# Retention scores inside halves of 256 tokens, with the first half's state carried to the second

## The chip, the core and the metric

The kernel runs on one core of one Trainium2 chip. The metric is the device time of one execution in microseconds (us). The kernel before was timed three times: 1077.37, 1076.7 and 1073.35 us, median 1076.7 us. One execution was also taken by the profiler. It took 1071.51 us, with a span of 1069.7 us from its first to its last recorded instruction, and every duration below is from that execution.

The core has five engines that work side by side, each through its own instructions in the order in which the program holds them: PE (matrix products into PSUM banks of 128x512), DVE (vector work), ACT (activations and scaled copies), POOL and SP (here almost only issuing DMAs). An instruction whose inputs are not ready holds up everything behind it on its own engine.

## The reference

One step of a decoder layer: a prompt of 512 tokens and eight sampled sequences of one token. The input is normalised, projected by one wide matrix, and goes through two branches, retention (RetNet) and RWKV-7, which are gated, merged, projected and normalised. The change touches retention alone, with 4 heads, keys of 256 and values of 512 elements:

```
def chunk(s, qkv):
    qc, kc, vc = qkv
    inner = jnp.einsum('bhid,bhjd->bhij', qc, kc) * dmask
    o = jnp.einsum('bhij,bhjv->bhiv', inner, vc) + jnp.einsum('bhid,bhdv->bhiv', qc * q_dec, s)
    s = chunk_dec * s + jnp.einsum('bhjd,bhjv->bhdv', kc * k_dec, vc)
    return s, o
```

The reference scans chunks of 128. Any chunk length gives the same result: a token's output is a decayed sum over all earlier tokens, either through scores against their keys or through a state that has summed them up. Wanted are the outputs `o` (normalised per token and head, then gated) and the last state `s`. All is float32.

## The kernel before

**Precision.** A float32 product is made of three products in the faster type F32R: each operand is split into a high part and the rest (`hi`, `lo`), and hi·hi, hi·lo and lo·hi are summed in PSUM. ACT makes the high part as a copy, DVE the rest as a difference.

**Weights.** `fetch` (L140) loads 512 KB of weights into a tile `raw`, of which there are three buffers. `weights` (L145) splits it: `whi` on ACT (L147), `wlo` on DVE (L148), two buffers each. So the split of one block of weights must wait until PE is through with the block two before it, and a load until all readers of the block three before it are done. `proj` (L160) then runs 48 products, 24 for each half of the tokens, into one of four banks named `ph`.

**One head of retention** (loop at `for h in range(H)`), in the order in which the code is written:

- `rope` for k and q: four blocks of weights, each followed by copies to `rx`; then on DVE three operations of 520 columns for each half of the head's dimension (L810 to L812) and a split.
- v: four blocks of weights of another shape (L838, 24 products of 512 columns each, into the four `ph` banks that stay open for all four). After the second and the fourth block the eight sampled tokens' v (`vsm`, L831) is made from the *unsplit* tiles `raw` of two blocks, so these two buffers stay taken until then. `vsm` lies in the only buffer of the bank `po`.
- Scores (L863): four blocks of 128 keys, block jt against queries 128·jt to 511, hence 512, 384, 256 and 128 columns wide; each is multiplied by the decay table `dmask` on DVE (L866) and split.
- Keys transposed back and scaled by their decay (`kt`, `dhi`, `dlo`, L882 to L884).
- `sampled`: the eight sampled sequences' states come from HBM by POOL's DMAs in tiles `tS` (four buffers, 1 MB each), are updated on ACT and DVE (L764, L765), go out again, and four rows of products end in the bank `po` (L770).
- Gates (`gs`), four blocks of weights.
- Outputs (L910): for each of four blocks of queries the products over all earlier key blocks, 30 in all; the final state (`st`, L921) from all four key blocks, 24 products; then the norm's factors `ort` by `rsqrt`, a chain of 13 small DVE instructions; `ot` transposed (L928) and gated into `gs` (L930); in the last step `sampled_out` makes a second factor `os` by the same chain, scales `po` by it on ACT into `on` (L782), which frees the bank `po`, and transposes `on` (`yas`, L785).

All banks but `ph` and `po` rotate through three buffers. Beside this, DVE works off RWKV's triangular solve (`tm` and `M`, L623 and L625, 62 pairs of up to 992 columns), which `advance` hands out by a running account of due work, and later the sampled RWKV heads.

**What sets the order.** The code is not issued as written. The tile framework plays the program through a model of the engines (`schedule_with_timeline_sim`) and puts each engine's instructions in the order in which they come up there, by readiness and by the order of the code. `tc.issue_after` and `after` add a few fixed precedences. Each edit can thus move instructions of any engine far from it.

Where a stage follows retention, RWKV's eight chunks run as chains of short products (L1025, L1034, L1040, L1043) among projections that fill the time.

Of the kernel before, what the change touches and what calls it, by code (L numbers as in the profile page):

```python
# [18 lines left out]
HT = 256  # L19
# [22 lines left out]
def constants():  # L42
    import numpy as np

    f = np.float32
    c = {}
    inv = (10000.0 ** (-np.arange(128) / 128)).astype(f)
    pos = np.concatenate([np.arange(T), np.full(B8, 4096)]).astype(f)
    ang = (pos[:, None] * inv[None, :]).astype(f)
    c["cos"] = np.ascontiguousarray(np.cos(ang).T.astype(f))  # L50
    c["sin"] = np.ascontiguousarray(np.sin(ang).T.astype(f))
    j = np.arange(128)[:, None]
    i = np.arange(T)[None, :]
    c["dmask"] = np.stack([np.where(i >= j, GAM[h] ** np.maximum(i - j, 0) / 16.0, 0.0) for h in range(H)], 1).astype(f)
    jj = np.arange(T).reshape(4, 128).T
    c["kdec"] = np.stack([GAM[h] ** (511 - jj) / 16.0 for h in range(H)], 1).astype(f)
    s = np.arange(64)[:, None]
    t = np.arange(64)[None, :]
    le, lt = (s <= t).astype(f), (s < t).astype(f)
    ev = np.concatenate([np.concatenate([le, -0.5 * lt], 1), np.concatenate([le, lt], 1)], 0)  # L60
    od = np.concatenate([np.concatenate([-0.5 * lt, le], 1), np.concatenate([lt, le], 1)], 0)
    c["gmask"] = np.concatenate([ev, od, ev, od], 1)
    r = np.ones((128, NT), f)
    r[:, 0:T:C] = 0.0
    r[:, T:] = 0.0
    c["reset"] = r
    ind = np.zeros((128, NPAIR, 16), f)
    for p in range(NPAIR):
        ind[:64, p, 2 * p] = 1.0
        ind[64:, p, 2 * p + 1] = 1.0  # L70
    c["ind"] = ind
    c["indT"] = np.ascontiguousarray(np.concatenate([ind.transpose(2, 1, 0)] * 2, 0))
    bd = np.zeros((128, 128), f)
    bd[:64, :64] = 1.0
    bd[64:, 64:] = 1.0
    c["bdiag"] = bd
    return c


def body(tc, A, O, dbg=None, upto="Z"):  # L80
# [11 lines left out]
    with es:  # L92
# [516 lines left out]
        pB.tile([128, 1280], F32R, tag="ihi", name="ihi")  # L609
        cos = pB.tile([128, NT], F32, tag="cos", name="cos")  # L610
        pool.dma_start(cos, A["cos"])
        sin = pB.tile([128, NT], F32, tag="sin", name="sin")
# [175 lines left out]
                              ps.rearrange("p (i b r) -> p i b r", i=4, b=4)[:, :, :, 0:2],  # L788
                              gs8[:, hs_, :].rearrange("p i (g b) -> p i b g", g=2), ALU.mult)

        OFF = [0, 512, 896, 1152]
        GBC = [0, 0, 0, 4, 8]
        for h in range(H):
            roped = {}
# [56 lines left out]
            qhi, qlo, _ = roped["q"]  # L851
            khi, klo, kf = roped["k"]

            dmask = pB.tile([128, T], F32, tag="dmask", name="dmask", bufs=1)
            (sp if h else pool).dma_start(dmask, A["dmask"][:, h, :])
            ihi = pB.tile([128, 1280], F32R, tag="ihi", name="ihi")
            ilo = pB.tile([128, 1280], F32R, tag="ilo", name="ilo")
            for jt in range(4):
                n = T - 128 * jt
                ps = bank("sc")  # L860
                seq = [(i, a_, b_) for i in range(2) for a_, b_ in ((khi, qhi), (khi, qlo), (klo, qhi))]
                for x, (i, a_, b_) in enumerate(seq):
                    pe.matmul(ps[:, 0:n], a_[:, i, 128 * jt:128 * jt + 128], b_[:, i, 128 * jt:T],  # L863
                              start=(x == 0), stop=(x == 5))
                s_ = pB.tile([128, T], F32, tag="s_", name="s_", bufs=1)
                dve.tensor_tensor(s_[:, 0:n], ps[:, 0:n], dmask[:, 0:n], ALU.mult)  # L866
# [12 lines left out]
            for jt in range(4):  # L879
                ps = bank("kt")  # L880
                for i in range(2):
                    pe.transpose(ps[:, 128 * i:128 * i + 128], kf[i][:, 128 * jt:128 * jt + 128], ident)  # L882
                act.activation(dhi[:, jt, :], ps[:, 0:256], AF.Copy, scale=kdec[:, h, jt:jt + 1])
                dve.scalar_tensor_tensor(dlo[:, jt, :], ps[:, 0:256], kdec[:, h, jt:jt + 1], dhi[:, jt, :], ALU.mult, ALU.subtract)  # L884
            po = sampled(h)

            gs = []
# [13 lines left out]

            oss = pB.tile([128, 4], F32, tag="oss", name="oss", bufs=2)
            ort = pB.tile([128, 4], F32, tag="ort", name="ort", bufs=2)
            ot = [x[:, i, :] for x in (pB.tile([128, 2, DV], F32, tag=t, name="ot") for t in ("qhi", "qlo")) for i in range(2)]
            for it in range(4):
                ps = bank("o")
                seq = [(jt, a_, b_) for jt in range(it + 1) for a_, b_ in ((ihi, vhi), (ihi, vlo), (ilo, vhi))]
                for x, (jt, a_, b_) in enumerate(seq):
                    o_ = OFF[jt] + 128 * (it - jt)
                    pe.matmul(ps, a_[:, o_:o_ + 128], b_[:, jt, :], start=(x == 0), stop=(x == len(seq) - 1))  # L910
                o = ot[it]
                act.activation(o, ps, AF.Square, accum_out=oss[:, it:it + 1])
                act.activation(o, ps, AF.Copy)
            rsqrt(ort, oss, 1.0 / DV, NORM_EPS)
            for it in range(4):
                act.activation(ot[it], ot[it], AF.Copy, scale=ort[:, it:it + 1])
            for i in range(2):
                ps = bank("st")
                seq = [(jt, a_, b_) for jt in range(4) for a_, b_ in ((dhi, vhi), (dhi, vlo), (dlo, vhi))]
                for x, (jt, a_, b_) in enumerate(seq):  # L920
                    pe.matmul(ps, a_[:, jt, 128 * i:128 * i + 128], b_[:, jt, :], start=(x == 0), stop=(x == 11))  # L921
# [408 lines left out]
```

## Time and profile before

| what | value |
|---|---|
| times of the kernel before | 1077.37, 1076.7, 1073.35 us |
| profiled execution, its time and its span | 1071.51 us, 1069.7 us |
| granted PE clock over the span | 0.992 |
| PE busy | 1042.0 us (97%), 8932 products |
| DVE busy | 785.2 us (73%) |
| ACT busy | 494.8 us (46%) |
| stage of retention | about 270 to 710 us of the span |
| in it, PE and DVE busy | 436.83 and 353.36 us of 440 |

A product's recorded time overlaps that of the next, since they are pipelined. What a product costs in a row of products is the distance from its start to the next one's start. The same holds in small for DVE: where instructions stand back to back, the next starts some 0.06 to 0.1 us before the recorded end of the one before. Rows named "waits" say who waited for whom; in the timeline, a bracket behind an instruction says how long its engine stood idle before it.

### The profile page before, as it was taken

How to read it: one execution, taken by the hardware profiler on the slowest of the kernel's cores; microseconds unless marked ns; L12 is line 12 of the kernel's file. 1: busy time of each engine (PE TensorE's matmuls, PEld its weight loads, DVE VectorE, ACT ScalarE, POOL GpSimd, SP SyncE). 2: the span in 40 equal slices, each digit the busy share in tenths (PEclk: the TensorE clock that was granted, in tenths of full speed). 3: DMA queues.
4: the chain of work that ended last, by engine and by line, in shares of the span. 5: the costliest groups of instructions: out<-in, count | busy, mean ns of one | idle time of the engine just before them, and what ended most of it. 6: DMA issues, size and time to landing. Idle time of an engine off the chain costs nothing.

```text
span 1069.7 us, 22049 instructions
## 1 busy us (share of the span) xinstructions
PE 1042.0 (97%) x8932; PEld 974.8 (91%) x8932; DVE 785.2 (73%) x1429; ACT 494.8 (46%) x973; POOL 79.5 (7%) x139
## 2 busy tenths in 40 slices
PE   7999999999999999999999999998999999999995
PEld 6999989999879788987989889898999999999995
DVE  6647989884499699949894698864777755666875
ACT  6744565544464543373445333354323224334554
POOL 2000110100300200010010000110001100000000
PEclk8999999999999999999999999999999999999998
DMA  5623488788943943493288633969996649643222
GB/s 182 179 80 99 122 191 223 188 246 228 330 160 90 327 146 99 144 319 103 86 310 229 230 115 112 328 198 330 309 283 214 171 145 302 206 119 100 81 59 81
DMA packets 239224, 199.45 MB, mean 186 GB/s; under 512 B 58988, under 2 KB 203225, under 8 KB 237970
## 3 DMA queue, kind: packets, MB, share of 16 engines
q1 hardware_dynamic: 225586, 149.60, 47.7%
q0 software_dynamic: 13376, 48.17, 13.2%
q8 instruction: 70, 1.15, 0.4%
q14 instruction: 32, 0.26, 0.1%
q10 hardware_dynamic: 160, 0.27, 0.1%
HBM read 137.70 MB, written 60.00 MB: 185 GB/s over the span
## 4 chain that ended last, share of the span: by engine, by line
PE 85%; DMA 6%; DVE 3%; ACT 2%; issue 1%; SPq 1%; POOL 0%; DVEq 0%; POOLq 0%; ACTq 0%
PE ph L160 58%; PE phv L838 8%; PE o L910 3%; PE st L921 2%; PE sc L863 1%; PE po L770 1%; PE g L506 1%; PE UO L1025 1%; DMA raw<-in_w_ple_gate_dram 1%; DMA raw<-in_w_in_dram 1%; DMA yalo<-YAd 1%; DMA BKt<-BKd 1%; DMA MBd<-mg 1%; PE vb L762 1%; PE vsm L831 1%
## 5 line engine op out<-in xcount | busy, mean ns | idle before, releaser
L160 PE MATMUL ph<-hhi,whi 128*128 128x256 f32 (+2 forms) x1296 | 370.5, 286 | 0.9 <-ACT hhi L282 0.4
L160 PE MATMUL ph<-hlo,whi 128*128 128x256 f32 (+2 forms) x1296 | 369.4, 285 | 0.2 <-DVE hlo L283 0.2
L160 PE MATMUL ph<-hhi,wlo 128*128 128x256 f32 (+2 forms) x1296 | 368.8, 285 | 0.5 <-DVE wlo L148 0.5
L160 PEld LDWEIGHTS ph<-hhi,whi 128*128 128x128 f32 x1296 | 244.2, 189 | 6.1 <-issue 1.7
L160 PEld LDWEIGHTS ph<-hhi,wlo 128*128 128x128 f32 x1296 | 245.0, 189 | 2.2 <-DVE wlo L148 0.7
L160 PEld LDWEIGHTS ph<-hlo,whi 128*128 128x128 f32 x1296 | 244.5, 189 | 1.9 <-DVE hlo L283 0.7
L147 ACT ACTIVATE whi<-raw 128x1024 fp32r<-128x1024 f32 x135 | 142.9, 1059 | 208.9 <-PE ph L160 154.2
L148 DVE TENSOR_TENSOR wlo<-raw,whi 128x1024 fp32r<-128x1024 f32 x135 | 164.8, 1221 | 86.4 <-ACT whi L147 85.4
L160 PE MATMUL ph<-yalo,whi 128*128 128x256 f32 (+1 forms) x256 | 72.4, 285 | 0.0
L160 PE MATMUL ph<-yahi,whi 128*128 128x256 f32 (+1 forms) x256 | 72.2, 284 | 0.0
L160 PE MATMUL ph<-yahi,wlo 128*128 128x256 f32 (+1 forms) x256 | 71.9, 285 | 0.0
L623 DVE TENSOR_TENSOR tm<-M 128x62 f32<-128x62 f32 (+30 forms) x62 | 52.9, 853 | 0.6
L625 DVE TENSOR_TENSOR M<-M,tm 128x62 f32<-128x62 f32 (+30 forms) x62 | 52.8, 852 | 0.6
L838 PE MATMUL phv<-whi,hhi 128*128 128x512 f32 x128 | 51.5, 403 | 0.0
L838 PE MATMUL phv<-whi,hlo 128*128 128x512 f32 x128 | 50.5, 395 | 0.0
L160 PEld LDWEIGHTS ph<-yalo,whi 128*128 128x128 f32 x256 | 48.1, 188 | 0.3
L160 PEld LDWEIGHTS ph<-yahi,whi 128*128 128x128 f32 x256 | 48.1, 188 | 0.2
L160 PEld LDWEIGHTS ph<-yahi,wlo 128*128 128x128 f32 x256 | 47.8, 188 | 0.3
L838 PE MATMUL phv<-wlo,hhi 128*128 128x512 f32 x128 | 46.8, 395 | 0.5 <-DVE wlo L148 0.5
L765 DVE SCALAR_TENSOR_TENSOR tS<-vb,ks,tS 128x512 f32<-128x512 f32 x64 | 44.1, 742 | 3.3 <-PE vb L762 3.3
L764 ACT ACTIVATE tS<-tS 128x512 f32<-128x512 f32 x64 | 35.0, 620 | 12.5 <-DMA tS<-in_state_ret_dram 12.4
L215 ACT ACTIVATE mg<-ph 128x256 f32<-128x256 f32 (+1 forms) x48 | 17.7, 378 | 41.2 <-PE ph L160 20.6
(454 smaller groups left out, 2120.0 us busy)
## 6 DMA issues: line engine op xcount, KB each, us to landing
raw<-in_w_in_dram SPq DMA_DIRECT2D x97, 512.0 KB, 5.0
tS<-in_state_ret_dram POOLq DMA_DIRECT2D x16, 1024.0 KB, 8.4
out_dram<-tS POOLq DMA_DIRECT2D x16, 1024.0 KB, 9.9
KR<-KRd SPq DMA_DIRECT2D x8, 1024.0 KB, 9.5
raw<-in_w_down_a_dram SPq DMA_DIRECT2D x16, 512.0 KB, 6.8
KRd<-KRS SPq DMA_DIRECT2D x16, 256.0 KB, 4.5
KRd<-GM SPq DMA_DIRECT2D x16, 256.0 KB, 4.8
BKt<-BKd SPq DMA_DIRECT2D x8, 512.0 KB, 9.9
```

The source lines that it names most:

```text
L147: cp = act.activation(hi, raw, AF.Copy)
L148: sb = dve.tensor_tensor(lo, raw, hi, ALU.subtract)
L160: m_ = pe.matmul(ps[:, 0:c1 - c0], w[:, k, :], r[:, k0 + k, c0:c1], start=(x == 0), stop=(x == n_ - 1))
L215: act.activation(g[:, c0:c1], ps, fn, scale=scale)
L506: ms = [pe.matmul(gs[2 * q + hh][:, c * 128:(c + 1) * 128], BK[hs_, 4 * q + c, :], KRS[hs_, 4 * q + c, :], start=True, stop=True) for q in ...
L623: dve.tensor_tensor(tv, M[:, 0:s, s:s + 1].to_broadcast([128, s, n]), M[:, s:s + 1, s + 1:C].to_broadcast([128, s, n]), ALU.mult)
L625: dve.tensor_tensor(M[:, 0:s, s + 1:C], M[:, 0:s, s + 1:C], tv, ALU.add)
L764: act.activation(S[:, b, :], S[:, b, :], AF.Copy, scale=GAM[h])
L765: last = dve.scalar_tensor_tensor(S[:, b, :], vb, ks[:, h, i, 4 * g + b:4 * g + b + 1], S[:, b, :], ALU.mult, ALU.add)
L838: m_ = pe.matmul(vps[jt], r[:, 2 * j + k, 128 * jt:128 * jt + 128], w_[:, k, :], start=(j == 0 and k == 0 and x == 0), stop=(j == 3 and k ...
L910: pe.matmul(ps, a_[:, o_:o_ + 128], b_[:, jt, :], start=(x == 0), stop=(x == len(seq) - 1))
L921: pe.matmul(ps, a_[:, jt, 128 * i:128 * i + 128], b_[:, jt, :], start=(x == 0), stop=(x == 11))
```

## The change

Scores are made inside halves of 256 tokens only: key blocks 0 and 1 against queries 0 to 255, blocks 2 and 3 against queries 256 to 511, so the four score blocks are 256, 128, 256 and 128 columns wide. The tables and tiles shrink to match (`dmask` 256 columns, `ihi` and `ilo` 768).

What the second half's queries get from the first half's keys now goes through the first half's state. Right behind the keys' transposes, 12 products (bank `st`) sum up key blocks 0 and 1; ACT copies the high part (`shi`), DVE makes the rest (`slo`, in the buffers `ro_k` of the rope's first step). At the outputs, 12 products (`oc`) of the two later query blocks with this state come first; ACT scales them by the query's decay (`qdec`, a new table loaded once) into `ot`. The output products are then 3, 6, 3 and 6. For the two later blocks DVE adds the inner part from PSUM to `ot` and ACT squares that into a scratch tile (`sqo`), where before ACT squared and copied straight from PSUM. The final state's products take key blocks 2 and 3 only, and DVE adds `shi` and `slo` in two steps, in the place of one copy on ACT. The tile `st` has one buffer, shared with rope's second step and the masked scores.

```diff
-        OFF = [0, 512, 896, 1152]
+        OFF = [0, 256, 384, 640]
+        qdec = pB.tile([128, H, 2], F32, tag="qdec", name="qdec")
+        pool.dma_start(qdec, A["qdec"])
...
             for jt in range(4):
-                n = T - 128 * jt
+                n = HT - 128 * (jt % 2)
...
-                    pe.matmul(ps[:, 0:n], a_[:, i, 128 * jt:128 * jt + 128], b_[:, i, 128 * jt:T],
+                    pe.matmul(ps[:, 0:n], a_[:, i, 128 * jt:128 * jt + 128], b_[:, i, 128 * jt:128 * jt + n],
...
+            vk = ((dhi, vhi), (dhi, vlo), (dlo, vhi))
+            shi = pB.tile([128, 2, DV], F32R, tag="shi", name="shi")
+            slo = [pB.tile([128, NT], F32R, tag="ro_k", name="slo", bufs=2)[:, 0:DV] for _ in range(2)]
+            for i in range(2):
+                ps = bank("st")
+                for x, (jt, (a_, b_)) in enumerate((jt, ab) for jt in range(2) for ab in vk):
+                    pe.matmul(ps, a_[:, jt, 128 * i:128 * i + 128], b_[:, jt, :], start=(x == 0), stop=(x == 5))
+                act.activation(shi[:, i, :], ps, AF.Copy)
+                dve.tensor_tensor(slo[i], ps, shi[:, i, :], ALU.subtract)
             po = sampled(h)
...
+            for it in (2, 3):
+                pss[it] = ps = bank("oc")
+                seq = [(i, a_, b_) for i in range(2) for a_, b_ in ((qhi, shi[:, i, :]), (qhi, slo[i]), (qlo, shi[:, i, :]))]
...
+            for it in (2, 3):
+                act.activation(ot[it], pss[it], AF.Copy, scale=qdec[:, h, it - 2:it - 1])
             for it in range(4):
                 ps = bank("o")
-                seq = [(jt, a_, b_) for jt in range(it + 1) for a_, b_ in ((ihi, vhi), (ihi, vlo), (ilo, vhi))]
+                seq = [(jt, a_, b_) for jt in range(it // 2 * 2, it + 1) for a_, b_ in ((ihi, vhi), (ihi, vlo), (ilo, vhi))]
...
-                act.activation(o, ps, AF.Square, accum_out=oss[:, it:it + 1])
-                act.activation(o, ps, AF.Copy)
+                if it < 2:
+                    act.activation(o, ps, AF.Square, accum_out=oss[:, it:it + 1])
+                    act.activation(o, ps, AF.Copy)
+                else:
+                    dve.tensor_tensor(o, o, ps, ALU.add)
+                    sqo = pB.tile([128, NT], F32, tag="ro_q", name="sqo", bufs=1)
+                    act.activation(sqo[:, 0:DV], o, AF.Square, accum_out=oss[:, it:it + 1])
...
-                seq = [(jt, a_, b_) for jt in range(4) for a_, b_ in ((dhi, vhi), (dhi, vlo), (dlo, vhi))]
...
+                for x, (jt, (a_, b_)) in enumerate((jt, ab) for jt in (2, 3) for ab in vk):
...
-                act.activation(st, ps, AF.Copy)
+                dve.tensor_tensor(st, ps, shi[:, i, :], ALU.add)
+                dve.tensor_tensor(st, st, slo[i], ALU.add)
```

The scheduler's order changes with it, from the first head's scores on. Three places matter below. In the rows of the changed kernel the line numbers are higher, by 1 up to L793, by 3 around the scores and by 26 behind them.

**DVE, end of head 0 and start of head 1.** `os` is the sampled tokens' norm factor, `nt` its scratch, `gs` the gated output, `m`, `klo`, `qlo` rope's work of head 1, `wlo` a split of weights. Before:

```order
L185 TENSOR_TENSOR nt<-nt,nv 128x1
L186 SCALAR_TENSOR_TENSOR os_4636<-nt,os_4636 128x1
L930 TENSOR_TENSOR gs<-ot,gs 128x512 x3
L811 TENSOR_TENSOR m_4789<-rx,sin 128x520
L930 TENSOR_TENSOR gs<-ot,gs 128x512
L787 TENSOR_TENSOR yaS<-yas,gs_66 128x4x4x2
L812 TENSOR_TENSOR m_4788<-m_4788,m_4789 128x520
L148 TENSOR_TENSOR wlo<-raw,whi 128x1024
```

and now:

```order
L817 TENSOR_TENSOR qlo<-m_4956,qhi 128x512
L186 TENSOR_TENSOR nt<-nt,nv 128x1
L752 COPY qz<-qs 128x8
L753 COPY qz<-qs 128x8
L187 SCALAR_TENSOR_TENSOR os_4655<-nt,os_4655 128x1
L788 TENSOR_TENSOR yaS<-yas,gs_66 128x4x4x2
L869 TENSOR_TENSOR s__5146<-sc,dmask 128x256
L872 TENSOR_TENSOR ilo<-s__5146,ihi 128x256
L869 TENSOR_TENSOR s__5157<-sc,dmask 128x128
L149 TENSOR_TENSOR wlo<-raw,whi 128x1024
```

The chain for `os` ended before the gating and before nearly all of head 1's rope, and the split in the last row is that of the first block of v's weights. Now the chain ends behind all of rope for k and q of head 1, and the split in the last row is that of the fourth block of v's weights, with head 1's first scores ahead of it. The split before that one, of the third block, stands 36 rows above `os`'s last row.

**PE, v of head 1.** `phv` is v, `vsm` the sampled tokens' v, `ot` and `yas` the transposes of head 0's outputs, `sc` head 1's scores. Before, with the last transposes of head 0 some 65 products earlier:

```order
L838 MATMUL phv<-whi,hhi 128x512
L838 MATMUL phv<-whi,hlo 128x512
L838 MATMUL phv<-wlo,hhi 128x512
L831 MATMUL vsm<-raw,hst 32x512 x4
L838 MATMUL phv<-whi,hhi 128x512
```

and now:

```order
L841 MATMUL phv<-whi,hhi 128x512
L841 MATMUL phv<-whi,hlo 128x512
L841 MATMUL phv<-wlo,hhi 128x512
L954 MATMUL ot<-ident,ot 128x128 x16
L786 MATMUL yas<-ident,on 128x128 x4
L834 MATMUL vsm<-raw,hst 32x512 x4
L866 MATMUL sc<-qhi,khi 128x256
L866 MATMUL sc<-qlo,khi 128x256
```

The first `vsm` stood behind 18 products of v; it now stands behind 72, that is three whole blocks, and behind all of head 0's transposes. Behind it come the 24 products of the scores, the second `vsm` and the fourth block of v. At the start of head 2 the order is the same, but for the `ot`, which are done earlier (the last four stand behind the first 18 products of v). Heads 0 and 3 have `vsm` behind 18 products of v, as before.

**PE, RWKV's first two chunks.** `UO` gets the first product of a chunk (from `KR`) and its last (from `DT`). Before:

```order
L1040 MATMUL dS<-SV,BKt 64x64 x16
L1043 MATMUL UO<-SV,DT 64x64 x16
L1025 MATMUL UO<-SV,KR 64x64 x32
L160 MATMUL ph<-hhi,whi 128x256
L160 MATMUL ph<-hlo,whi 128x256
```

and now:

```order
L1066 MATMUL dS<-SV,BKt 64x64 x16
L1069 MATMUL UO<-SV,DT 64x64 x16
L161 MATMUL ph<-hhi,whi 128x256
L161 MATMUL ph<-hlo,whi 128x256
L161 MATMUL ph<-hhi,wlo 128x256
```

The second chunk's first products followed the first chunk's last ones at once; now 36 products of a projection stand between them.

More of the change, by code (lines that the diff above doesn't have):

```diff
@@ L55, in constants @@
     jj = np.arange(T).reshape(4, 128).T
+    c["qdec"] = np.stack([GAM[h] ** (np.arange(-255.0, 1.0).reshape(2, 128).T) for h in range(H)], 1).astype(f)
     c["kdec"] = np.stack([GAM[h] ** (511 - jj) / 16.0 for h in range(H)], 1).astype(f)
@@ L608, in body @@
         pB.tile([128, 4, DV], F32R, tag="vlo", name="vlo")
-        pB.tile([128, 1280], F32R, tag="ihi", name="ihi")
+        pB.tile([128, 768], F32R, tag="ihi", name="ihi")
         cos = pB.tile([128, NT], F32, tag="cos", name="cos")
@@ L852, in body @@
             khi, klo, kf = roped["k"]
[L854 to L857, printed above, removed]
+            dmask = pB.tile([128, HT], F32, tag="dmask", name="dmask", bufs=1)
+            (sp if h else pool).dma_start(dmask, A["dmask"][:, h, 0:HT])
+            ihi = pB.tile([128, 768], F32R, tag="ihi", name="ihi")
+            ilo = pB.tile([128, 768], F32R, tag="ilo", name="ilo")
             for jt in range(4):
-                n = T - 128 * jt
+                n = HT - 128 * (jt % 2)
                 ps = bank("sc")
@@ L903, in body @@
             ort = pB.tile([128, 4], F32, tag="ort", name="ort", bufs=2)
+            pss = {}
+            for it in (2, 3):
+                pss[it] = ps = bank("oc")
+                seq = [(i, a_, b_) for i in range(2) for a_, b_ in ((qhi, shi[:, i, :]), (qhi, slo[i]), (qlo, shi[:, i, :]))]
+                for x, (i, a_, b_) in enumerate(seq):
+                    pe.matmul(ps, a_[:, i, 128 * it:128 * it + 128], b_, start=(x == 0), stop=(x == 5))
             ot = [x[:, i, :] for x in (pB.tile([128, 2, DV], F32, tag=t, name="ot") for t in ("qhi", "qlo")) for i in range(2)]
+            for it in (2, 3):
+                act.activation(ot[it], pss[it], AF.Copy, scale=qdec[:, h, it - 2:it - 1])
             for it in range(4):
                 ps = bank("o")
-                seq = [(jt, a_, b_) for jt in range(it + 1) for a_, b_ in ((ihi, vhi), (ihi, vlo), (ilo, vhi))]
+                seq = [(jt, a_, b_) for jt in range(it // 2 * 2, it + 1) for a_, b_ in ((ihi, vhi), (ihi, vlo), (ilo, vhi))]
                 for x, (jt, a_, b_) in enumerate(seq):
@@ L918, in body @@
                 ps = bank("st")
-                seq = [(jt, a_, b_) for jt in range(4) for a_, b_ in ((dhi, vhi), (dhi, vlo), (dlo, vhi))]
-                for x, (jt, a_, b_) in enumerate(seq):
-                    pe.matmul(ps, a_[:, jt, 128 * i:128 * i + 128], b_[:, jt, :], start=(x == 0), stop=(x == 11))
+                for x, (jt, (a_, b_)) in enumerate((jt, ab) for jt in (2, 3) for ab in vk):
+                    pe.matmul(ps, a_[:, jt, 128 * i:128 * i + 128], b_[:, jt, :], start=(x == 0), stop=(x == 5))
                 st = pB.tile([128, DV], F32, tag="s_", name="st", bufs=1)
-                act.activation(st, ps, AF.Copy)
+                dve.tensor_tensor(st, ps, shi[:, i, :], ALU.add)
+                dve.tensor_tensor(st, st, slo[i], ALU.add)
                 pool.dma_start(O[2][0, 0, h, 128 * i:128 * i + 128, :], st)
```

## The prediction

> **What bounds the kernel now.** First the profile's page, for which engine is busy and where. The 40 digits of a row are tenths of busy time in slices of 26.7 us; retention lies in slices 11 to 27.
>
> ```profile
> span 1069.7 us, 22049 instructions
> PE 1042.0 (97%) x8932; PEld 974.8 (91%) x8932; DVE 785.2 (73%) x1429; ACT 494.8 (46%) x973; POOL 79.5 (7%) x139
> PE   7999999999999999999999999998999999999995
> DVE  6647989884499699949894698864777755666875
> ```
>
> PE shows 9 in every slice but the first, one behind retention and the last; DVE shows 9 in seven of retention's seventeen. Next the sums of that stage (length, then the busy time of PE, PEld, DVE, ACT and POOL, the granted clock, DMA share, GB/s), and the waits of PE, asked stretch by stretch (in all, times, longest):
>
> ```profile
> 270.00:710.00 440.00, 436.83 (x2991) 384.13 (x2990) 353.36 (x561) 206.50 (x404) 42.06 (x63) 1.00 0.59 193
> PE vsm L831 <- issue: 2.6, 1, 2.6
> PE phv L838 <- DVE wlo L148: 0.5, 1, 0.5
> PE UO L1025 <- ACT Ot L1056: 3.4, 3, 2.7
> ```
>
> The two waits in the middle are all that retention has, in head 0; from 370 to 710 us PE waits for nothing. The last row is RWKV's, behind retention. So retention is bound by PE, and a product taken away there is time gained, as long as the others keep handing PE its inputs in time. DVE has 86.6 us of slack in the 440, but slack in a stage says nothing of one stretch.
>
> **The products removed.** What a product costs is the distance between starts. Head 0's scores:
>
> ```profile
> 316.72 0.39 PE L863 MATMUL sc<-qhi,khi 128*128 128x512 f32 x1
> 317.41 0.34 PE L863 MATMUL sc<-qhi,khi 128*128 128x384 f32 x1
> 317.94 0.28 PE L863 MATMUL sc<-qlo,khi 128*128 128x256 f32 x1
> 318.06 0.28 PE L863 MATMUL sc<-qhi,klo 128*128 128x256 f32 x1
> 318.18 0.28 PE L863 MATMUL sc<-qhi,khi 128*128 128x256 f32 x1
> 321.74 0.22 PE L863 MATMUL sc<-qhi,khi 128*128 128x128 f32 x1
> 322.36 0.34 PE L160 MATMUL ph<-hhi,whi 128*128 128x264 f32 x1
> ```
>
> Three of 512 columns stand between 316.72 and 317.41, 0.23 us each; three of 384 take 0.177, one of 256 takes 0.12, and six of 128 take 0.62 together, 0.103 each. Per head six products go from 512 to 256 (0.66 us) and six from 384 to 128 (0.44): 1.1 us, **4.4 us** in four heads. The other counts stay: outputs 30 against 18 + 12, states 24 against 12 + 12.
>
> The Trainium skill (TensorE: Matmul & The Clock Gate, "Wait — 56ns, not 53.3ns?") gives a warm product columns over 2.4 GHz plus 2.5 ns, 55.6 ns at 128 columns. The rows do not agree at 128 (0.103 us), so the narrow blocks save less; by the page the term would be an estimated 5.1 us.
>
> **The work added to DVE** is eight operations of 512 columns a head (two `slo`, two adds to `ot`, four for `st`), some 0.62 us each by the gating below, 5 us; narrower masks and splits give back about 1. On ACT as many copies go as come. I cost these 4 us a head at nothing as work, since DVE has 86.6 us left; uncovered they would be 16. Their price is in the order, which they and the earlier products have moved.
>
> **The hand-over from head 0 to head 1.** Here the chain for `os` now ends behind all of head 1's rope, and the first `vsm` stands behind three blocks of v. Three things hang on it: `on` frees the only bank `po`, `vsm` writes there, and `vsm` alone still holds two of three `raw` buffers, so that the load of v's fourth block waits for it. Before, that was hidden:
>
> ```profile
> 391.62 1.06 PE L831 MATMUL vsm<-raw,hst 128*32 128x512 f32 x8
> 392.71 0.90 SPq L142 DMA_DIRECT2D raw<-in_w_in_dram  x2
> L782 ACT ACTIVATE on<-po,os x4: 668/679/693, 377.7 to 701.1; 128x512 f32<-128x512 f32 x4
> 380.98 0.60 PE L785 MATMUL yas<-ident,on 128*128 128x128 f32 x4
> 379.99 1.03 PE L928 MATMUL ot<-ident,ot 128*128 128x128 f32 x8
> DMA to landing us min/median/max: 3.7/4.9/13.6
> L147 ACT ACTIVATE whi<-raw 128x1024 fp32r<-128x1024 f32 x135 | 142.9, 1059 | 208.9 <-PE ph L160 154.2
> L148 DVE TENSOR_TENSOR wlo<-raw,whi 128x1024 fp32r<-128x1024 f32 x135 | 164.8, 1221 | 86.4 <-ACT whi L147 85.4
> ```
>
> The first two rows show it: SP sends two loads right as `vsm` ends, with 78 products of v and head 1's first scores left to cover them (18 of 96 had run). The landing row is that of `raw` in retention. For DVE's pace, a dense stretch:
>
> ```profile
> 377.15 0.16 DVE L184 TENSOR_TENSOR nt<-os 128x1 f32<-128x1 f32 x1
> 377.34 0.16 DVE L185 TENSOR_TENSOR nt<-nt,nv 128x1 f32<-128x1 f32 x1
> 377.62 1.28 DVE L930 TENSOR_TENSOR gs<-ot,gs 128x512 f32<-128x512 f32 x2
> 399.28 0.69 DVE L810 TENSOR_TENSOR m<-rx,cos 128x520 f32<-128x520 f32 x1
> 399.89 1.17 DVE L623 TENSOR_TENSOR tm<-M 128x980 f32<-128x980 f32 x1
> 400.98 0.69 DVE L812 TENSOR_TENSOR m<-m,m 128x520 f32<-128x520 f32 x1
> 401.59 1.21 DVE L148 TENSOR_TENSOR wlo<-raw,whi 128x1024 fp32r<-128x1024 f32 x1
> 402.72 1.17 DVE L625 TENSOR_TENSOR M<-M,tm 128x980 f32<-128x980 f32 x1
> 403.81 0.68 DVE L814 TENSOR_TENSOR qlo<-m,qhi 128x512 fp32r<-128x512 f32 x1
> 404.42 0.16 DVE L751 COPY qz<-qs 128x8 f32<-128x8 f32 x1
> ```
>
> Start to start: rope 0.61 us, a solve step 1.09, a split of weights 1.13, of q 0.61, a gating about 0.62, a small step 0.2 after one it depends on, about 0.1 (my guess, between 0.07 and 0.2) among others.
>
> Count from PE's start of v's first block. A block is 24 × 0.23 = 5.5 us. The third block's split needs the first block's buffers, free at 5.5; with `whi` 1.06 and `wlo` 1.22 it ends at 7.8 at the earliest. Behind it on DVE, up to the last `os`: 7 rope steps (4.3), 4 splits of k and q (2.4), 5 solve steps (5.5), 4 gatings (2.5), 15 small steps (2.0) and two copies (0.1), 16.8 together: 24.6. Then `on` 0.68, `yas` 0.6, `vsm` 1.0, the load 4.9, `whi` and `wlo` 2.3, and five hand-overs of 0.1: 34.6. PE's own work until then is three blocks (16.6), 16 `ot` (1.6), `yas` (0.4), twice `vsm` (2.0), 24 scores (12 × 0.12 + 12 × 0.103 = 2.7) and two products of block four that need no `wlo` (0.5): 23.8. **PE waits 10.8 us.** The load at its fastest makes that 9.6; the third split may come as late as 11.5 before PE feels it by itself, and makes it 14.5.
>
> **From head 1 to head 2** the third split is followed by only 3 rope steps, 2 splits, 4 solve steps and 4 small ones up to `os`, at most 8 us: 15.8, `on` 16.5, while PE reaches `yas` at 17. From there `yas` 0.4, `vsm` 1.0, load 4.9, splits 2.3, hand-overs 0.4: 26.0, against PE's 22.2 with only four `ot` in it. **3.8 us**; 2.6 with the fastest load, 5.5 with a late split. Heads 0 and 3 keep `vsm` early: nothing.
>
> **The clock.** A PE that waits this long loses more. At the start, where PE also waits:
>
> ```profile
> 7.30:10.70 3.40, 1.68 (x13) 1.19 (x11) 3.23 (x16) 2.98 (x5) 1.26 (x2) 1.00 1.05 372
> 10.70:17.50 6.80, 6.05 (x25) 5.46 (x26) 6.59 (x21) 5.18 (x13) 0.00 (x0) 0.50 0.62 177
> ```
>
> After a 3.4 us stretch with PE half idle the granted clock is 0.50 for 6.8 us, worth 3.4 us to a full PE. Head 1's wait surely does this (about 7 us ahead of `yas`, 4 behind the scores), head 2's by even chance: 3.4 + 1.7 = **5.1 us**, from 0 to 8. The Trainium skill (same page, "What's actually happening") has the clock halve after an idle window of some 3.4 us; the trace agrees.
>
> **RWKV's second chunk** waited 2.7 us for `Ot` in ACT's queue (the `UO` row); 36 products of 0.12, 4.3 us, now cover that: **−2.7**, between that and 0.
>
> **Sum:** −4.4 + 10.8 + 3.8 + 5.1 − 2.7 = +12.6 us. The profiled execution took 1071.5, so 1084.1 by its own time. It lies 5.2 us under the median of the runs, 1076.7, which I take as base: **1089 us**.
>
> **Rivals.**
> *The hand-over holds.* If `os` came before v's third block ended, everything would be covered and the removed work alone count: −4.4 − 2.7, 1070 us. For it: PE waited for none of this before. Against: no work can leave the 16.8 us, and 7.8 is already the earliest start. It decides only if DVE needs under 6 us there (13.8 + 10 for the rest of the chain is PE's 23.8). 0.13.
> *Only DVE's own sum counts.* If the fourth block's load did not wait for `vsm`, its split would still stand 19.2 us of DVE work behind the third (16.8, then `yaS`, two masks and one split of them, about 1.3 by 0.61 for 512 columns, and itself 1.13), at 27 against PE's 23.8: 3.2 us, too short for the clock and nothing in head 2. −3.9: 1073 us. Against: the two rows 391.62 and 392.71. 0.18.
> *The `st` add blocks DVE.* This one is worse yet. The second `st` needs the first one's store, and it now waits on DVE, with all splits behind it, where ACT waited before.
>
> ```profile
> DMA to landing us min/median/max: 2.2/3.8/12.7
> ```
>
> Between the two stand 5.1 us of DVE work (two rope steps, a split, two solve steps, small ones), which covers 3.8 but not 12.7, and POOL now sends two 1 MB loads ahead of both stores of heads 0 and 1. At the longest landing DVE, and the chain with it, slips 8 us: 1097. It decides from a landing of 5 us. 0.14.
>
> **How the numbers follow.** My forecast has 0.55. 0.5% (5.4 us) is what a measurement of this kernel can tell from no change. Slower by more, over 1082.1: nearly all of the forecast (0.51), the blocked DVE (0.14) and a little of the sum case (0.03), 0.68. Faster by more, under 1071.3: the first rival, 0.13. Same: 0.19. The forecast's own range runs from its terms' ends, −4.4 + 9.6 + 2.6 + 0 − 2.7 = +5 to −4.4 + 14.5 + 5.5 + 8 = +24: 1082 to 1100. To hold eight in ten it takes in the second rival: 1073 to 1100.
>
> **What would show it.** PE waits of about 11 and 4 us around the first `vsm` and the first products of v's fourth block in heads 1 and 2, SP's `raw` right behind `vsm`, granted clock 0.50 there, no wait at the second chunk's `UO`; scores of 256 columns at 0.12 us. It is wrong if PE's digits in retention stay at 9 and head 1 takes no longer than before.

## The result

| | median us | lowest to highest | runs |
|---|---|---|---|
| before | 1075.03 | 1070.09 to 1077.37 | 4 |
| changed | 1101.77 | 1101.3 to 1109.37 | 4 |

The changed kernel takes 1.0262 times as long (95% interval 1.023 to 1.0294), some 27 us more. The forecast had slower, with 1089 us and a range up to 1100. So the sign was right, the loss that was forecast (12.6 us) is about half of what came, and the time lies 2 us outside the range. Of all runs below one, of the kernel with all three edits, took 2036.27 us; its median is of the other eleven.

The profiled execution of the changed kernel is the one of 1109.37 us, 7.6 us above its median, and that of the kernel before (1071.51 us) lies 3.5 us under its own. So the two traces differ by 38 us and the medians by 27. The traces tell where time went; how much, the timed runs below.

### The profile page after: what moved, and what is told of

It is laid out like the page before. It is cut to its first block, busy times and chain, and to the rows that moved or that the text cites. A ratio compares the mean times of both kernels' runs of the same rounds, so it can differ in the third digit from the quotient of the medians.

```text
span 1107.6 us, 22088 instructions
## 1 busy us (share of the span) xinstructions
PE 1048.3 (95%) x8932; PEld 977.1 (88%) x8932; DVE 799.3 (72%) x1461; ACT 492.7 (44%) x973; POOL 79.9 (7%) x140
## 4 chain that ended last, share of the span: by engine, by line
PE 70%; DMA 13%; issue 7%; DVE 5%; ACT 2%; SPq 2%; POOL 0%; POOLq 0%; DVEq 0%; ACTq 0%
PE ph L161 52%; PE phv L841 4%; DMA out_dram<-tS 2%; DMA raw<-in_w_in_dram 2%; DMA out_dram<-st 2%; PE g L507 1%; PE UO L1051 1%; DMA yalo<-YAd 1%; PE po L771 1%; SPq L630 1%; DMA xn<-in_x_prompt_dram 1%; DMA BKt<-BKd 1%; DMA o<-OSd 1%; ACT whi L148 1%; PE o L931 1%
## 5 line engine op out<-in xcount | busy, mean ns | idle before, releaser
L161 PE MATMUL ph<-ybhi,whi 128*128 128x264 f32 (+1 forms) x128 | 37.4, 293 | 9.1 <-ACT ybhi L1176 9.1
```

Source lines behind the costliest of these rows:

```text
L161: m_ = pe.matmul(ps[:, 0:c1 - c0], w[:, k, :], r[:, k0 + k, c0:c1], start=(x == 0), stop=(x == n_ - 1))
```

## The profile after

First the page: the span, the busy times, and the digits of PE and DVE in 40 slices.

```profile
span 1107.6 us, 22088 instructions
PE 1048.3 (95%) x8932; PEld 977.1 (88%) x8932; DVE 799.3 (72%) x1461; ACT 492.7 (44%) x973; POOL 79.9 (7%) x140
PE   7999999999899978999999899999998996999995
DVE  6647988873699597869884598874676863566775
```

PE now has dips in retention (8 from 277, 7 and 8 from 388 to 443 us, 8 around 620) and in the stage behind it (8 from 831, 6 from 914 us). DVE has 32 instructions and 14 us more, and shows 9 in six slices instead of ten. What PE waited for, asked stretch by stretch (in all, times, longest); the first three rows are head 0 to 1, the next three head 1 to 2, then head 3, then two behind retention:

```profile
PE yas L786 <- ACT on L783: 7.4, 1, 7.4
PE vsm L834 <- ACT whi L148: 1.9, 1, 1.9
PE ot L954 <- DVE gs L956: 1.7, 1, 1.7
...
PE vsm L834 <- ACT whi L148: 1.3, 1, 1.3
PE yas L786 <- ACT on L783: 0.9, 1, 0.9
PE sc L866 <- DVE s__6168 L869: 0.5, 1, 0.5
...
PE phv L841 <- DVE wlo L149: 5.1, 1, 5.1
...
PE ph L161 <- ACT ybhi L1176: 9.1, 1, 9.1
PE dS L1066 <- DVE SV L1064: 3.2, 1, 3.2
```

Head 0 to 1 waits 11.0 us and head 1 to 2 waits 2.7, which were forecast as 10.8 and 3.8. The 5.1 of head 3 and the 12.3 behind retention were not forecast. The sums of the stretches (length, busy PE, PEld, DVE, ACT, POOL, granted clock, DMA share, GB/s) show retention, the long wait, what follows it, head 2's short waits, the wait for `SV` and what follows it, and what follows the wait for `ybhi`:

```profile
270.00:710.00 440.00, 417.64 (x2842) 363.58 (x2841) 344.63 (x542) 188.30 (x370) 37.69 (x57) 0.98 0.55 179
409.00:417.00 8.00, 0.62 (x5) 0.38 (x6) 7.00 (x20) 2.05 (x4) 0.00 (x0) 0.55 0.35 131
417.00:421.00 4.00, 4.00 (x22) 2.00 (x22) 0.31 (x2) 0.00 (x0) 0.00 (x0) 0.63 0.01 1
515.00:524.00 9.00, 6.39 (x45) 4.30 (x48) 6.81 (x14) 2.78 (x5) 0.00 (x0) 1.00 0.39 117
846.70:850.10 3.40, 0.85 (x8) 0.65 (x6) 1.33 (x2) 0.00 (x0) 0.00 (x0) 0.99 0.27 69
850.10:856.90 6.80, 6.17 (x75) 5.94 (x76) 5.46 (x9) 2.14 (x3) 0.88 (x1) 0.50 0.90 272
931.00:936.00 5.00, 4.12 (x20) 3.82 (x20) 2.59 (x3) 1.36 (x3) 0.00 (x0) 0.56 0.91 288
```

In the wait of 7.4 us the granted clock is already down to 0.55, and the 4 us behind it have 0.63; behind the 9.1 us it is 0.56, and behind head 3's 5.1 us (628 to 634 us) 0.70. The waits of about 1 us in head 2 leave 1.00. But the wait of 3.2 us for `SV` was enough to halve the clock for 6.8 us. The Trainium skill (TensorE: Matmul & The Clock Gate, "What's actually happening") has the clock halve after an idle window of some 3.4 us. The trace agrees for the long waits, but in the 3.4 us ahead of 850.1 PE was busy for 0.85 us and the clock halved all the same; so a kernel can lose clock by shorter waits than that.

Where in the program the changed kernel falls back, by the starts of the same products in both traces (of `vsm` the last product):

| product | before | changed | later by |
|---|---|---|---|
| second `vsm` of head 0 | 310.5 | 313.7 | 3.2 |
| of head 1 | 406.4 | 425.3 | 18.9 |
| of head 2 | 502.4 | 524.2 | 21.8 |
| of head 3 | 622.3 | 647.8 | 25.5 |
| RWKV's first `UO` | 722.7 | 753.8 | 31.1 |
| RWKV's last `so` | 880.3 | 917.6 | 37.3 |
| end of the span | 1069.7 | 1107.6 | 37.9 |

Between heads 0 and 1 the fall-back grows by 15.7 us. Not all of it is lost there: the new order has 39 products of scores in that stretch instead of 20, some 2 us of work that the kernel before does later. Two rows are larger than their waits explain. From head 3's `vsm` to `UO` the fall-back grows by 5.6 us, while PE waits for nothing in the end of retention. From `UO` to `so` it grows by 6.2 us, with a wait of 3.2 (before: 3.4).

## The experiments

All times are medians, each beside runs of the kernel before on the same chip (medians 1075.7 to 1076.6 us).

**The narrow scores alone**, in the kernel before, to price the first term by itself.

```diff
-        OFF = [0, 512, 896, 1152]
+        OFF = [0, 256, 384, 640]
...
-                n = T - 128 * jt
+                n = HT - 128 * (jt % 2)
...
-                    o_ = OFF[jt] + 128 * (it - jt)
+                    o_ = OFF[jt] + (128 * (it - jt) if it // 2 == jt // 2 else 0)
```

> The kernel before with the scores' widths of the change alone: 256, 128, 256, 128 columns, the masking and splitting as wide; the products of the outputs stay 30 a head, but those of the second half with the first half's keys take a block of scores that is there, so that part of the outputs is left out of the computation. No state is made earlier, no work is added. Theory (the prediction's term): -4.4 us on PE and nothing else, 1075.0 - 4.4 = 1070.6 us, 1068 to 1073. Rival, the scores' time was cover for what DVE and ACT do there, and a wait takes its place: 1074 to 1078. Rival, narrower blocks cost their rows' 0.39 to 0.28 us each and save more: below 1067.

1071.34 us against 1075.72, ratio 0.9957 (0.9941 to 0.9974): 4.4 us, the forecast's term. The gain is real, and the rest of the change loses some 31 us beside it.

**The chain for `os`.** The trace of the changed kernel showed that the forecast had the place right and not the reason. DVE's rows in head 0 to 1:

```profile
380.34 0.16 DVE L179 TENSOR_SCALAR nv<-oss 128x4 f32<-128x4 f32 x1
...
388.67 0.69 DVE L948 TENSOR_TENSOR st<-st,shi 128x512 f32<-128x512 f32 x1 [2.63 <-DMA out_dram<-st]
...
392.09 0.15 DVE L185 TENSOR_TENSOR nt<-ort 128x4 f32<-128x4 f32 x1
392.16 1.22 DVE L149 TENSOR_TENSOR wlo<-raw,whi 128x1024 fp32r<-128x1024 f32 x1
...
403.81 0.16 DVE L187 SCALAR_TENSOR_TENSOR ort<-nt,ort 128x4 f32<-128x4 f32 x1
403.89 0.15 DVE L179 TENSOR_SCALAR nv<-os 128x1 f32<-128x1 f32 x1
403.95 0.69 DVE L814 TENSOR_TENSOR m<-rx,sin 128x520 f32<-128x520 f32 x1
...
408.02 0.15 DVE L182 TENSOR_SCALAR os<-os 128x1 int32<-128x1 int32 x1
...
415.99 0.15 DVE L187 SCALAR_TENSOR_TENSOR os<-nt,os 128x1 f32<-128x1 f32 x1
```

The norm of the outputs (`ort`) takes 23 us for 13 rows of 0.15 us, since the plan lays larger operations between most of them, and DVE once waits 2.63 us for the store of the first `st`. The sampled tokens' norm (`os`) starts 0.08 us behind the last of them: both use the same scratch `nv` and `nt`, one buffer each, through the helper `rsqrt`. `po`, on which `os` depends, had its last product at 369. So the sampled norm waited for a scratch tile of 128x4, and not for its turn behind the rope, as the next run shows; it then had its own 13 rows spread in the same way over 12 us. ACT's row for what follows, in the same trace:

```profile
416.18 0.69 ACT L783 ACTIVATE on<-po,os 128x512 f32<-128x512 f32 x1 [0.95 <-DVE os L187]
```

One edit takes the wait away.

```diff
-            rsqrt(os2[:, 1:2], os2[:, 0:1], 1.0 / DV, NORM_EPS)
+            rsqrt(os2[:, 1:2], os2[:, 0:1], 1.0 / DV, NORM_EPS, tag="ns")
```

> The changed kernel with one edit: the sampled tokens' norm gets scratch of its own (two tiles of 128x1), where it shared one pair of tiles with the norm of the outputs. Nothing is left out. The theory of the hand-over: `os` comes late because its 13 small rows on DVE wait for the outputs' 13, which use the same pair, and are then spread over 12 us of other DVE work. Freed of them, `os` stands right behind `po`, `on` frees the bank some 20 us earlier, and the waits at head 0 to 1 (7.4 for yas, 1.9 for vsm and about 3 beside them, 12.5 in all) and at head 1 to 2 (3.1) go: 1101.8 - 15.6 = 1086 us, 1083 to 1090. Rival, DVE has simply too much to do in this stage: the waits only move to wlo or the scores, 1099 to 1103. Rival, the loss lies elsewhere (a store of the states, the stage behind retention) and the hand-over is covered by a later wait: 1095 to 1102.

1081.93 us, ratio 1.006 (1.004 to 1.0081): 20 us back by one argument, four more than expected. The first norm is now the sampled one, and `on` follows 44 us earlier; DVE's rows and ACT's:

```profile
365.65 0.15 DVE L179 TENSOR_SCALAR nv<-os 128x1 f32<-128x1 f32 x1 [0.77 <-ACT on L781]
...
374.57 0.16 DVE L179 TENSOR_SCALAR nv<-oss 128x4 f32<-128x4 f32 x1
```

```profile
371.84 0.69 ACT L783 ACTIVATE on<-po,os 128x512 f32<-128x512 f32 x1
```

The waits for `on` are gone from both hand-overs, while the DVE work that the change adds is all there (799.4 us busy). Head 3's wait of 5.1 us and the one of 3.2 us for `SV` are gone with them, so the 20 us are not the hand-overs' alone. But behind retention PE waited longer than ever:

```profile
PE ph L161 <- ACT ybhi L1176: 12.4, 1, 12.4
```

**The same edit in the kernel before**, to see whether it is simply a good edit.

> The kernel before with scratch of its own for the sampled norm and nothing else. Nothing is left out. Theory: there the two norms follow each other within 8 us and hide behind PE's work, so the edit is worth nothing: 1074 to 1077 us; the shared scratch costs only in the changed order. Rival, the edit is an improvement by itself, and the 20 us that it brought in the changed kernel say little of the change: below 1071.

1076.54 us, ratio 0.9997 (0.9972 to 1.0022). In the old order the two norms stand side by side and cost nothing; only the changed order makes the shared scratch a wait.

**The store of the state.** Head 3's wait of 5.1 us, by the chain of waits of the changed kernel (start, us, what):

```profile
601.84 8.47 DMA TTd<-M
...
610.94 1.80 POOL S__7017 L676 x4
...
613.04 12.50 DMA out_dram<-st
...
625.57 0.06 DVE m L814
...
626.18 1.23 DVE wlo L149
```

The store of head 2's second `st` stands on POOL's queue behind four loads that wait for `TTd`, and then takes 12.5 us to land. Its buffer `s_` is also that of the rope's second step, which DVE cannot start, and `wlo` is behind it. This is the mechanism of the third rival, further on, in head 2's stores, and through the rope instead of the second `st`. The slow store itself is not new. In the kernel before it stands behind the same four loads and lands after 12.7 us, the longest landing that the prediction quotes; only DVE came to the rope's step so late that it stood 0.65 us for it. The same step of DVE before, and now:

```profile
605.05 0.70 DVE L811 TENSOR_TENSOR m<-rx,sin 128x520 f32<-128x520 f32 x1 [0.65 <-DMA out_dram<-st]
...
625.57 0.70 DVE L814 TENSOR_TENSOR m<-rx,sin 128x520 f32<-128x520 f32 x1 [9.64 <-DMA out_dram<-st]
```

```diff
-                st = pB.tile([128, DV], F32, tag="s_", name="st", bufs=1)
+                st = pB.tile([128, NT], F32, tag=("s_", "ro_q")[i], name="st", bufs=1)[:, 0:DV]
```

> The changed kernel with the second half of the final state written to the scratch of the queries' rope instead of the one buffer that both halves, the scores and the rope's second step share. Nothing is left out. Theory: the one buffer, held by a store that took 12.5 us behind the loads of S_ on POOL's queue, made head 3's wait for wlo (5.1 us at 622.0), and DVE's idle 2.6 us at 386 (second half's add behind the first half's store): both go, 1101.8 - 5 to 8 = 1094 to 1097 us. Rival, the profile's 5.1 us is an accident of that one execution: 1100 to 1103. Rival, the queries' rope waits in the same way, only later: 1100 to 1105.

1098.82 us, ratio 1.022 (1.0188 to 1.0252): 3.0 us, less than expected, and not clearly more than nothing (the interval overlaps the changed kernel's 1.023 to 1.0294). The 5.1 us are gone from the trace, but head 1 to 2 now waits about as long as head 0 to 1:

```profile
PE yas L786 <- ACT on L783: 11.5, 2, 6.1
```

**The end behind retention.** The wait for `ybhi` was first read as an accident of SP's order.

```diff
-                sp.dma_start(src, YBd[:, :, cols].rearrange("k r n -> r k n"))
+                pool.dma_start(src, YBd[:, :, cols].rearrange("k r n -> r k n"))
```

> The changed kernel with the loads of yb issued from POOL's queue instead of SP's. Nothing is left out. Theory: the 9.1 us in which PE waits for ybhi at 921.8 come from SP, where the first load of yb stands between the last two stores of UAd (before: ahead of the last but one); from POOL the load goes as soon as YBd is written and the wait goes: 1101.8 - 9 to 11 = 1091 to 1093 us. Rival, YBd itself is late (its store lands when the load is sent anyway) and the wait stays: 1100 to 1103. Rival, the profiled execution, 7.6 us above the median, is the only one with this wait: 1100 to 1103 too, but then the profile of this run and its time differ from the profile of the changed kernel by those 9 us.

1103.55 us, ratio 1.025 (1.022 to 1.028): nothing gained, this theory fell. PE waited as long for the loads behind those moved:

```profile
PE xt L1190 <- DMA xn<-in_x_prompt_dram: 11.1, 2, 9.7
```

So the place of this one load in its queue does not set the time; the loads behind it come as late. This run's code is the changed kernel's up to that load, and its trace shows the other waits again (8.2 us for `on`, 4.0 in head 3, 3.1 for `SV`), so they are no accident of one execution. What differs between the kernels is when PE runs out of other work. With own scratch the chain from RWKV's last transposes reads (start, us, what):

```profile
890.14 0.60 ACT So L1160
890.75 0.28 issue
891.03 4.43 DMA out_dram<-So
895.46 6.88 DMA yb<-YBd
...
902.36 1.07 ACT ybhi L1176
...
903.45 1.24 DVE yblo L1177
```

This chain of 13.6 us must be covered by projections that are left. The table counts them, from the same rows of each trace: projection products (0.12 us each) between head 3's second `vsm` and RWKV's first `UO`, and between its last `so` and the first product of `ybhi`.

| kernel | products `vsm` to `UO` | `UO` starts | last `so` | products `so` to `ybhi` | `ybhi` | end |
|---|---|---|---|---|---|---|
| before | 568 | 722.7 | 880.3 | 135 | 897.0 | 1069.7 |
| changed | 626 | 753.8 | 917.6 | 35 | 931.2 | 1107.6 |
| own scratch | 674 | 734.2 | 889.8 | 8 | 903.5 | 1080.3 |
| own scratch, last head as before | 628 | 731.1 | 884.6 | 66 | 894.8 | 1068.4 |
| own scratch, `So` elsewhere | 674 | 738.8 | 895.5 | 8 | 902.9 | 1078.5 |
| own scratch, store moved | 628 | 728.4 | 881.8 | 66 | 892.0 | 1068.0 |
| all three edits | 628 | 732.7 | 886.1 | 66 | 895.7 | 1070.5 |

In the changed kernel the end of retention takes longer for its own chains, and PE fills that time with 58 products that belong behind it. PE is busy, and nothing shows in its waits; but RWKV starts 58 x 0.12 = 7 us later (less 1.4 us for scores that are narrower or done earlier), and between `UO` and `so` PE takes in 42 more. At the end these 100 products are missing, 35 instead of 135. With own scratch it is 106 and 21, and 8 are left.

A product that is taken early costs nothing by itself, since it need not be done later. The loss is the wait that its absence uncovers. From `UO` on, the kernel before takes 347.0 us and the one with own scratch 346.1, which was first read as the end following RWKV's start. The other rows do not bear this out: the changed kernel takes 353.8 us, the last four 337 to 340, and with scratch and store moved RWKV starts 5.7 us later than before and the span ends 1.7 us earlier. Three kinds of runs tried this.

*Less to fill with*, in the kernel before:

```diff
-            for (j, c0, c1), ps in zip(HV, proj(w_in[:, col(c_, m)], hhi, hlo)):
+            for (j, c0, c1), ps in zip(HV, mm([(*weights(w_in[:, col(c_, m)]), 0, KT // 2 if c_ == O_MB and m > 3 else KT)], hhi, hlo)):
```

> The kernel before, with half of the products left out in four of the eight gates for the merge that run beside the end of retention and RWKV: 96 products, some 11.5 us of PE's time; their half of the sum over the input is left out of the computation. Theory of the chain: the end is set as much by the chain from retention's end through RWKV's chunks to yb as by PE's work, and the two are balanced in the kernel before; the taken-away work turns into a wait for ybhi, and the time falls by 1 to 5 us only: 1070 to 1074.5. Rival, PE's work alone sets the end, as the 97% say: 1063 to 1065.

1073.32 us against 1076.55, ratio 0.9962 (0.9936 to 0.9988): 3.2 us for 11.5 us of taken-away work. So PE's work was not the only bound there, as the theory said; but the wait came up at another link than it had, the loads of RWKV's third chunk:

```profile
PE UO L1025 <- DMA SV<-Vd: 5.3, 1, 5.3
PE ph L160 <- ACT mg L215: 1.8, 1, 1.8
```

*A shorter chain at the end*, with own scratch and in the kernel before:

```diff
-            So = pC.tile([64, 16, C], F32, tag="gsq", name="So", bufs=1)
...
-                act.activation(So[:, 8 * q:8 * q + 8, :].rearrange("v h k -> v (h k)"), ps[0:64], AF.Copy)
-            pool.dma_start(O[3][0, 0].rearrange("h v k -> v h k"), So)
+                So = gp.tile([128, NT], F32, tag="mg", name="So", bufs=2)[0:64, 0:8 * C]
+                act.activation(So, ps[0:64], AF.Copy)
+                pool.dma_start(O[3][0, 0, 8 * q:8 * q + 8].rearrange("h v k -> v h k"), So.rearrange("v (h k) -> v h k", k=C))
```

> The changed kernel with scratch of its own for the sampled norm, and RWKV's final state So written through the gates' two buffers, whose memory nothing behind needs. Nothing is left out. Theory: at the end of RWKV PE waits 12.6 us on the chain So, its store's landing (4.4 us), the load of yb (6.9 us) into the memory that So frees, ybhi, yblo; without the store's landing the wait shrinks by 4 to 5 us: 1077 to 1078 us. Rival, another buffer of RWKV holds the same memory, or the load is queued behind loads of weights on SP: 1081 to 1083.

> The kernel before with RWKV's final state written through the gates' buffers and nothing else. Nothing is left out. Theory: there 135 products, 16.2 us, stand behind RWKV's last transposes and cover the chain to ybhi (16.7 us from the last transpose to the first product that uses it, without a wait), so a shorter chain is worth nothing: 1074 to 1078 us. Rival, the chain was what set the end there too: 1068 to 1072, and the edit's 4.8 us in the changed kernel say nothing of the change.

With own scratch 1077.13 us (0.9992, 0.9969 to 1.0014), 4.8 less than without this edit (on another chip; the ratio was 1.006), and the wait for `ybhi` has halved:

```profile
PE ph L161 <- ACT ybhi L1176: 6.1, 1, 6.1
```

In the kernel before 1075.77 (1.0008, 0.9988 to 1.0029): nothing. So the chain at the end sets the time once its cover is spent, and not before.

*The last head as before the change*, the others as changed:

```diff
+            old = h == H - 1
...
-                n = HT - 128 * (jt % 2)
+                n = T - 128 * jt if old else HT - 128 * (jt % 2)
...
-            for it in (2, 3):
+            for it in () if old else (2, 3):
...
-                if it < 2:
+                if it < 2 or old:
```

> The changed kernel with scratch of its own for the sampled norm, and besides the last head computed as before the change: wide scores, outputs of 30 products, one state of 24; heads 0 to 2 as changed. Nothing is left out. Theory of the chain: from RWKV's first product to the end it took 346 to 348 us in the kernel before, with own scratch, with the state store moved and with narrow scores, so the end is set by when retention's last head lets RWKV start; with own scratch that was 11.5 us later than before, because the last head's sampled products came 13.5 us later. With the last head as before it starts 10 to 14 us earlier, and three heads keep their 1.1 us: 1081.9 - 8 to 12 = 1070 to 1074 us. Rival, the 12.6 us for ybhi arise in the stage behind retention and stay: 1081 to 1085 (1.1 us of gain is given back). Rival, the wider scores bring a new wait at the hand-over to the last head: above 1085.

1070.9 us, ratio 0.9936 (0.9903 to 0.9969). The time is the one expected, the reason is not: RWKV starts only 3.1 us earlier, and the last head's sampled products come no earlier (last one at 698.1; 696.8 with own scratch alone). What else is better in its trace are the 66 products behind `so` and a chain of 10.2 us instead of 13.6, with a wait for `ybhi` of 2.0 us.

**Scratch and store together**, all four heads as changed.

> The changed kernel with scratch of its own for the sampled norm and the second half of the final state in the scratch of the queries' rope. Nothing is left out. In the planned order 628 products of gates and fills stand between the last head's second vsm and RWKV's first product, against 674 with own scratch alone and 568 before, and 66 instead of 8 behind RWKV's last transposes. Theory: what counts is how many later products PE takes in ahead of RWKV's start (0.12 us each): RWKV starts 46 products, 5.5 us, earlier than with own scratch alone, and the wait for ybhi falls from 12.6 to about 13.6 - 66 x 0.12 = 5.7 us: 1081.9 - 5.5 to 7 = 1075 to 1076.5 us. Rival, moving the store is worth the 3 us it brought without own scratch: 1079 us. Rival, it no longer matters: 1081 to 1083.

1068.91 us, ratio 0.9946 (0.9926 to 0.9966): faster than the kernel before, and lower than any of the three theories had it (the lowest 1075). RWKV starts 5.8 us earlier than with own scratch alone, as forecast. The chain at the end shrank by itself to 10.2 us: SP's order now has the load of `yb` ahead of the last store of `UAd` and of two loads of weights. Which of the two, the cover or the shorter chain, brought how much was not separated here. Its wait for `ybhi`, and the page:

```profile
PE ph L161 <- ACT ybhi L1176: 2.0, 1, 2.0
```

```profile
PE 1039.2 (97%) x8932; PEld 970.8 (91%) x8932; DVE 798.4 (75%) x1461; ACT 493.8 (46%) x973; POOL 79.9 (7%) x140
PE   7999999999999999999999999999999998999995
```

**All three edits:**

> The changed kernel with scratch of its own for the sampled norm, the second half of the final state in the scratch of the queries' rope, and RWKV's final state written through the gates' buffers. Nothing is left out; all four heads are as changed. Theory: as with the first two edits, RWKV starts 46 products earlier than with own scratch alone, and the chain behind it is 6.2 us shorter (7.4 instead of 13.6 us from so to ybhi), which the 66 products cover: 1077.1 - 5.5 - 6 = 1064 to 1068 us, faster than before by about 1%. Rival, only PE's own work is then left, which the change has made 4.4 us less: 1070 to 1072. Rival, a new wait takes its place: 1075 or more.

1068.68 us, ratio 0.9939 (0.9916 to 0.9961). The third edit adds nothing that can be told from the two; the wait for `ybhi` had only 2.0 us left to give. The time lies between the theory's (1064 to 1068) and the first rival's (1070 to 1072), in which PE's own work is all that is left, and does not decide between them.

## Why the prediction was half right

- **Scores, −4.4 us:** right; measured 4.4 by themselves.
- **DVE's added work, nothing as work:** right. With scratch and store apart all of it is still there, and the kernel is faster than before.
- **Head 0 to 1, 10.8 us:** right in place and size; 11.0 us of waits. That `os` comes late and holds `po`, `vsm` and `raw` is shown by the run with own scratch, in which these waits are gone. The cause of the lateness was not seen: the text took the order of DVE's rows as given and said of the first rival that "no work can leave the 16.8 us". The shared scratch was what put the 13 rows there.
- **Head 1 to 2, 3.8 us:** right, 2.7 us of waits. (For the upper end the text has 5.5; its own late split, 3.7 us later, gives 3.8 + 3.2 = 7.0, since 0.5 us of it are slack. The range would have reached 1102.)
- **The clock, 5.1 us:** too large for these two places. Most of the half clock lay inside the wait, where PE loses nothing by it. By the rows from 409 to 421 us the loss is an estimated 1.8 us (busy time by the missing share of the clock), and nothing in head 1 to 2. By the same estimate 2.2 us were lost in head 3 (1.92 us busy at 0.77, then 6.00 at 0.70), 3.1 behind the wait for `SV` and 2.1 around the one for `ybhi` (1.13 at 0.71, then 4.12 at 0.56), all in places that the forecast did not have.
- **"Heads 0 and 3 keep `vsm` early: nothing":** wrong for head 3. `vsm` was early, but 5.1 us came by the store of `st`. The third rival had this mechanism, and the landing of 12.7 us from the trace of before, but did not ask which store that was: it was head 2's second. It priced it only for the second `st` of heads 0 and 1 (there DVE stood 2.6 us for it), and as an alternative to the forecast instead of beside it.
- **RWKV, −2.7:** the wait at the second chunk's `UO` is gone, as forecast, and one of 3.2 us for `SV` stands in its place; why, was not tried. But the stage was costed by that one wait, and this step failed most: PE waited 9.1 us for `ybhi`, where before it waited for nothing. The forecast read "bound by PE" off the digits and summed only waits that were there. It did not count the products that cover the chain from RWKV's end to `ybhi`, nor what the new order leaves of them, 35 of 135. Both could be read off the trace of before and the two planned orders. Before, PE works through the whole chain, which ends just as its cover does (PE's chain of waits, and ACT's last `ybhi`):

```profile
880.56 16.21 PE ph L160 x135
...
894.68 1.21 ACT L1150 ACTIVATE ybhi<-yb 128x1024 fp32r<-128x1024 f32 x2 [1.08 <-DMA yb<-YBd]
```

  None of these 135 products behind the last `so` needs `ybhi`, and the first that does follows at 897.0: 16 us of work cover a chain that elsewhere took 7 to 14.

The sum of the two traces can be closed by the page. Before, PE stood idle for 27.7 us of the span (1069.7 − 1042.0), now for 59.3: 31.6 more. It was busy 6.3 us longer with the same 8932 products, though the narrower scores take 4.4 off: 10.7 us. Some 9 of these are the slower clock: the 1.8, 2.2, 3.1 and 2.1 us estimated above and 1.7 in head 0 (3.40 us busy at 0.50 from 293.7 us), less 1.7 that the kernel before lost behind its wait for `UO` (3.35 at 0.50). Of idle time the forecast had 11.9 us (10.8 + 3.8 − 2.7). The two hand-overs gave 13.7, about as forecast; head 3's 5.1 and the 9.1 for `ybhi` are the two failed steps, each with its clock. These three make 27.9 of the 31.6; the wait for `SV` is set off by the one for `UO` that is gone, and the rest lies in small waits.

The traces differ by 38 us and the medians by 27, so some of this belongs to the one profiled execution, 7.6 us above its median; why, is open. The 3.2 us that it lost ahead of head 0's second `vsm` are of that kind: in the run with the load of `yb` moved, whose code is the same up to there, this product starts at 309.0, and before at 310.5.

A reading of the prediction that changes nothing in its sum: DVE shows 9 in eight of retention's slices, not seven.

**Still open:** why own scratch alone moved the last head's sampled products behind some hundred more products of gates (408 instead of 311 between `vsm` and the first product of `po`). That the plan did it is seen in its order; which of its rules did, was not tried. Nor was it tried why moving the store as well brings them forward again.

## What to carry to other kernels

Before a change that reorders work, look for small tiles with one buffer that two chains share (the scratch of a helper called twice): in one order they cost nothing, in another they tie a chain that was ready to one that is late. And a bounding engine that never waits is no proof that a stage is not late: where a scheduler fills gaps with later work, compare when the next stage's first instruction starts and how much filling is left behind its last one. Cost a change on both, the engine's work and that chain.

## What the runs showed of the hardware

A store of 256 KB took 12.5 us to land when four loads of the sampled states, 512 KB each, had been issued right ahead of it on the same queue; in the kernel before it took 12.7 us in the same place. Of the two `st` stores of head 0 in the changed kernel, the first, issued right behind a load of 1 MB, took 5.8 us, and the second, with the last load 9 us ahead, 2.3:

```profile
DMA to landing us min/median/max: 2.3/4.1/5.8
```

That the loads ahead make the difference was not tried by itself; other queues were moving data too.

In the run with less to fill, PE, which is busy 97% of the span of the kernel before, lost some 11.5 us of its work for a gain of 3.2.
